# A two-layer hybrid trunk: the attention's queries and keys are projected with channels in the rows

## Chip, cores and metric

One of the eight cores of a Trainium2 chip runs the whole program. The metric is the device time of one execution in microseconds (us).

## What is computed

The input is 256 positions of 2048 channels. Each of two layers normalises it, projects it once to 7692 columns, and gives slices of the result to three mixers: a gated convolution module (31 taps, layer norm, a 512x512 projection), a gated DeltaNet with 6 heads, and an attention with 12 heads of 64 channels. The concatenated outputs go through one output projection and are added to the residual. The change concerns the attention's queries and keys:

```python
x1, x2, rest = x[..., :8], x[..., 8:16], x[..., 16:]          # per head, x is q or k
x = concatenate([x1 * c - x2 * s, x2 * c + x1 * s, rest])     # c, s: tables by position
s = einsum("qe,ke->qk", q, k) * 64 ** -0.5
```

Only 16 of a head's 64 channels are rotated, channel j with channel j+8.

## The kernel before

**Main chain.** All large projections are one sequence of jobs (`project`, line 466), run one after the other on TensorE. A job multiplies 16 blocks of 128 input channels; a block is a `unit` (line 439). Weights arrive as f32 (`raw`), ScalarE rounds them to a high part (`whi`, line 191), VectorE forms the low part (`wlo`, line 199), and each unit adds three products. There are two ways to place a unit. With `chan` false the activations (`HT`) are the stationary operand and the weight rows stream: 6 matmuls of 384 columns for a 384 wide block, the result has positions in the rows. With `chan` true the weights are stationary and the 256 positions stream: 9 matmuls of 256 columns, the result has channels in the rows. Three slots hold `whi` and three hold `wlo`, one for each chunk of two units.

**Order of jobs in a layer**: decay columns and DeltaNet keys, conv inputs, DeltaNet queries, values and gate, then for each half i of the heads attention queries, keys and values (AQ, AK, AV), then the conv gate (CG, 512 columns), the conv module's own projection (`wpw`, 4 units; its `then` is `conv_out`), the attention gates (AG), and the output projection.

**Everything else** is small tasks, interleaved with the chain. Small matmuls and transposes write to four PSUM tiles, `MIX` (named mix0 to mix3, also 123 to 126), which a task gets and puts back. `Plan` (line 70) is a list scheduler that runs when the program is built: with estimated costs it takes, of all tasks, the one that can start first, and on a tie the one with the lowest priority number. It fixes the order of every engine's instructions, and each engine then runs in that order. Attention pairs (`att_pair`) have priority 16, the conv module (`conv_a`) 20.

**The conv module** runs on VectorE for most of a layer (31 taps x 4 blocks). When the last tap is done, a chain follows: four transposes per half of the positions (`trs`, line 239), copies with sums and squares with sums on ScalarE, a power on GpSimd (`gpow`, line 248), scaling on VectorE, eight transposes back, scale, tanh and product, and the split into YT, which the `wpw` job reads.

**Queries and keys** (`heads_in`): the 384 columns come with positions in the rows and are scaled by `rstd` (or `half` for q) as they leave PSUM. VectorE rotates the 16 channels per head with four small operations per half of the positions, TensorE turns three blocks of 128 channels with two transposes each, and ScalarE copies the result.

Of the kernel before, what the change touches and what calls it, by code (L numbers as in the profile page):

```python
# [11 lines left out]
F32 = mybir.dt.float32  # L12
# [3 lines left out]
ALU = mybir.AluOpType  # L16
# [5 lines left out]
S = 256  # L22
DEPTH = 2
H = 6
AH = 12
HD = 64
CW = 31
KB = D // 128
NT = S // 128
# [4 lines left out]
AQ, AK, AV, AG = 4620, 5388, 6156, 6924  # L34
# [6 lines left out]
P_CW, P_DW, P_DB, P_LW, P_LB, P_GN, P_AL, P_DT, PCOLS = 16, 88, 212, 216, 220, 224, 225, 231, 237  # L41


PAD = (32, 16)


class Event:
# [128 lines left out]
def hybrid_trunk(ctx, tc, x, x_t, w_in, conf_pw_w, w_out, params, final_norm_w, rope, lnc, out):  # L176
    nc = tc.nc
    cp = ctx.enter_context(tc.tile_pool(name="consts", bufs=1))
# [5 lines left out]
    plan = Plan()  # L184


    def act(out_, in_, func=AF.Copy, scale=1.0, bias=0.0, accum=None):
        n_ap = sum(not isinstance(v, (int, float)) for v in (scale, bias)) + (accum is not None)
        kw = {} if accum is None else {"accum_out": accum}
        return ("act", 95 + _free(out_) / 1.2 + 93 * n_ap,  # L190
                lambda: nc.scalar.activation(out_, in_, func, bias=bias, scale=scale, **kw))  # L191
# [44 lines left out]
    def trs(*jobs):  # L236
        def emit():
            for o, a in jobs:
                nc.tensor.transpose(o, a, ident)  # L239
        return ("pe", 107.0 * len(jobs), emit)  # L240
# [14 lines left out]
        return Slots([(pool or sp).tile([128, cols], dt, name=f"{name}{i}", tag=f"{name}{i}") for i in range(n)])  # L255

    lncs = cp.tile([128, 384], F32, name="lncs")
    ropes = cp.tile([128, NT, 32], F32, name="ropes")
    cp.tile([128, PAD[0]], F32, name="pad0")
    HT = [cp.tile([128, KB, S], F32R, name=f"HT{i}") for i in range(2)]  # L260
    YT = [cp.tile([128, KB, S], F32R, name=f"YT{i}") for i in range(2)]
# [5 lines left out]
    S768 = many(14, 768, "b768_")  # L267
# [4 lines left out]
    S256 = many(4, 256, "b256_")  # L272
# [3 lines left out]
    MIX = many(4, 512, "mix", pool=pp)  # L276
# [29 lines left out]
    RSTD = [cp.tile([128, NT], F32, name=f"rstd{l}") for l in range(DEPTH + 1)]  # L306
    sums = cp.tile([128, NT], F32, name="sums")
    cp.tile([128, PAD[1]], F32, name="pad1")
    HALF = [cp.tile([128, NT], F32, name=f"half{l}") for l in range(DEPTH)]
    ROW = [cp.tile([128, S], F32, name=f"row{l}") for l in range(DEPTH)]  # L310
    misc_ready = [Event() for _ in range(DEPTH)]
    conv_ready = [Event() for _ in range(DEPTH)]
# [68 lines left out]
    def load_x(j):  # L381

        c0, n = X_PIECES[j]
        buf = yield ("get", S768)
        xs = buf[:, :NT * n].rearrange("p (t c) -> p t c", t=NT)
        yield ("dma", 128 * NT * n * 4 / 330.0, lambda: nc.sync.dma_start(
            xs, xf[:, c0:c0 + n].rearrange("(t p) c -> p t c", p=128)))
        plan.spawn(sums_x(j, xs, buf), 3)
        if j == len(X_PIECES) - 1:
            nc.sync.dma_start(lncs, lnc)  # L390
            nc.sync.dma_start(ropes, rope.rearrange("(t p) c -> p t c", p=128))

    def sums_x(j, xs, buf):
        yield from square_sums(0, j, [xs[:, t] for t in range(NT)], nsq0[j])
# [113 lines left out]
    rstd_ready = [Event() for _ in range(DEPTH)]  # L508
    final_ready = [Event() for _ in range(NT)]
    row_ready = [Event() for _ in range(DEPTH)]  # L510

    def square_sums(l, j, xs, ev):
        for t in range(NT):
# [35 lines left out]
    def finish_norm(l, evs, t0=0, t1=NT):  # L549
        for e in evs:  # L550
            yield ("wait", e)
        r = RSTD[l][:, t0:t1]
        if l == DEPTH:
            yield ts(r, SSQ[l][:, t0:t1, len(LAST_PIECES) - 1], 1.0 / D, sums[:, t0:t1], ALU.mult, ALU.add)
        else:
            yield ("dve", 90.0, lambda: nc.vector.tensor_reduce(r, SSQ[l][:, t0:t1], AX.X, ALU.add))
            yield ts(r, r, 1.0 / D, 1e-6, ALU.mult, ALU.add)
        yield gpow(r, r, pw_neg[:, :t1 - t0])
        if l == DEPTH:
            yield ("set", final_ready[t0])  # L560
            return
        yield ts(HALF[l], r, 0.125, None, ALU.mult)
        yield ("set", rstd_ready[l])
        ps = yield ("get", MIX)
        yield trs(*((ps[:, t * 128:(t + 1) * 128], r[:, t:t + 1].to_broadcast([128, 128])) for t in range(NT)))
        yield copy(ROW[l], ps[:, :S])
        yield ("put", MIX, [ps])
        yield ("set", row_ready[l])


    def layer(l):
        par = PAR[l]
        cw, dw = par[:, P_CW:P_CW + 72], par[:, P_DW:P_DW + 4 * CW]
        rstd, half = RSTD[l], HALF[l]
        y_ready = [Event() for _ in range(KB)]
        jobs = []

        def evac(acc, n, dsts, scale=None):
            yield ("wait", rstd_ready[l])
            for t in range(NT):  # L580
                yield act(dsts[t], acc[t][:, :n], scale=(rstd if scale is None else scale)[:, t:t + 1])


        conf = {k: Event() for k in ("pw", "b", "g")}
# [240 lines left out]
        def keys():  # L825
            for h in range(H):
                yield ("wait", gd["head"]["k", h])
            yield ("wait", gd["g"])
            yield ts(ssk, ssk, 4e-6, None, ALU.add)
            yield gpow(rk, ssk, pw_neg)  # L830
            yield tt(ivk, ssk, rk, ALU.mult)
            yield tt(fm, rk, rk, ALU.mult)
            yield tt(fm, fm, be.rearrange("p t h -> p (t h)"), ALU.mult)
            yield tt(ko, fm[:, :H], eg[:, 0], ALU.mult)
            yield ("set", gd["f"])
# [190 lines left out]

        at, at_have = {}, {(w, i): Event() for w in "qk" for i in range(2)}

        def heads_in(which, i):
            def then(acc):  # L1030
                raw = yield ("get", S768)
                tl = raw.rearrange("p (t c) -> p t c", t=NT)
                sc = rstd if which != "q" else half
                yield from evac(acc, 384, [tl[:, t] for t in range(NT)], sc)
                yield ("put", ACC, [acc])
                if which == "v":
                    at["v", i] = tl
                    for hp in range(3):
                        plan.spawn(att_pair(i, hp), 16 + 0.1 * hp)
                    return  # L1040
                ra, rb = yield ("get", S256, 2)
                ra_, rb_ = (r[:, :96].rearrange("p (h e) -> p h e", e=16) for r in (ra, rb))
                for t in range(NT):
                    v = tl[:, t].rearrange("p (h e) -> p h e", e=HD)
                    cc = ropes[:, t:t + 1, 0:16].to_broadcast([128, 6, 16])
                    ns = ropes[:, t:t + 1, 16:24].to_broadcast([128, 6, 8])
                    ss = ropes[:, t:t + 1, 24:32].to_broadcast([128, 6, 8])
                    yield tt(ra_, v[:, :, 0:16], cc, ALU.mult)
                    yield tt(rb_[:, :, 0:8], v[:, :, 8:16], ns, ALU.mult)
                    yield tt(rb_[:, :, 8:16], v[:, :, 0:8], ss, ALU.mult)  # L1050
                    yield tt(v[:, :, 0:16], ra_, rb_, ALU.add)
                yield ("put", S256, [ra, rb])
                buf = yield ("get", S768)
                dst = buf.rearrange("p (h s) -> p h s", s=S)
                for b in range(3):
                    ps = yield ("get", MIX)
                    yield trs(*((ps[:, t * 128:(t + 1) * 128], tl[:, t, b * 128:(b + 1) * 128])
                                for t in range(NT)))
                    yield act(dst[:, b, :], ps[:, :S])
                    yield ("put", MIX, [ps])  # L1060
                yield ("put", S768, [raw])
                at[which, i] = dst
                yield ("set", at_have[which, i])
            return then

        def att_pair(i, hp):
# [169 lines left out]
        def inp(c0, n, then, prio, chan=False):  # L1236
            order = full if l or jobs else halved
            jobs.append((HT, h_ready[l], win, c0, n, order, then, prio, None, chan))
# [7 lines left out]
                inp(c0 + 384 * i, 384, gdn_block(w, i), 6, True)  # L1246
        inp(GZ, 384, z_block, 6)
        for i in range(2):
            for w, c0 in (("q", AQ), ("k", AK), ("v", AV)):
                inp(c0 + 384 * i, 384, heads_in(w, i), 7)  # L1250
        inp(CG, 512, conv_gate, 6, True)
        cs_ready = [conf["pw"]] * KB
        jobs.append((YT, cs_ready, wpw, 0, 512, full[:2], conv_out, 6, None, True))
# [2 lines left out]
        for j, (c0, n) in enumerate(pieces):  # L1256
            mode = "last" if last and j == len(pieces) - 1 else False
            jobs.append((YT, y_ready, wout, c0, n, [(4 * i, 4) for i in range(4)] if mode else full, (last_residual if last else residual)(j),
                         4, load_residual(j), mode))
        bg = [(keys(), 11), (gdn_out(), 13)] + [(scores(b), 14) for b in range(4)] + [(state(i), 12) for i in range(2)]  # L1260
        return jobs, bg

    setup_consts()
# [38 lines left out]
def _rope_table():  # L1302

    half = 8
    inv = np.float32(500000.0) ** (-np.arange(half, dtype=np.float32) / np.float32(half))
    ang = np.arange(S, dtype=np.float32)[:, None] * inv.astype(np.float32)[None, :]
    c, s = np.cos(ang), np.sin(ang)
    return np.concatenate([c, c, -s, s], axis=1).astype(np.float32)


def _pattern_logs():
# [26 lines left out]
```

## Time and profile before

| what | value |
|---|---|
| median of 3 runs | 972.93 us (972.45 to 974.32) |
| the profiled execution | 972.88 us, its span 971.2 us |
| TensorE matmul busy | 958.6 us, 99% of the span |
| VectorE busy | 748.1 us, 77% |
| ScalarE busy | 550.8 us, 57% |
| GpSimd busy | 48.6 us, 5% |
| granted TensorE clock | 0.997 of full |

Matmul spans overlap their neighbours, so the busy share alone does not say how fast the columns flow. The chain of waits gives a number of matmuls and the time from the first to the last of a stretch, and that quotient is the cost of one.

### The profile page before, as it was taken

The numbers are of one execution on the slowest core, as the hardware profiler recorded it, in microseconds if no ns is written. First come the engines' busy times: TensorE is split into PE (matmuls) and PEld (weight loads), VectorE is DVE, ScalarE is ACT, GpSimd is POOL, SyncE is SP. The second block draws the span as 40 slices with busy tenths as digits, with TensorE's granted clock in tenths as the row PEclk, the third lists the DMA queues.
The fourth block names the chain that finished last, engine by engine and source line by source line (L and its number), as shares of the span: only waits on it lengthen the run. The fifth ranks groups of instructions, "written<-read, shape, count | busy, mean of one in ns | idle before, by whom it ended". The sixth has DMA issues, their size and how long they took to land.

```text
span 971.2 us, 19060 instructions
## 1 busy us (share of the span) xinstructions
PE 958.6 (99%) x7259; PEld 937.3 (97%) x7259; DVE 748.1 (77%) x1519; ACT 550.8 (57%) x1079; POOL 48.6 (5%) x70
## 2 busy tenths in 40 slices
PE   8999999999999999999999999999999999999996
PEld 8999999999999999999899999999899999999996
DVE  7697799999999666655558768999999976666672
ACT  7774355446685764554456634564466767544551
POOL 1002100200010000000000020002000100000000
PEclk9999999999999999999999999999999999999998
DMA  9865565644445535776666555556344556467772
GB/s 325 261 201 170 175 192 183 187 148 146 148 138 173 183 114 185 222 244 219 215 194 196 196 168 172 188 181 196 123 149 142 151 186 203 125 194 218 221 252 88
DMA packets 67037, 179.01 MB, mean 184 GB/s; under 512 B 8000, under 2 KB 12224, under 8 KB 66944
## 3 DMA queue, kind: packets, MB, share of 16 engines
q1 hardware_dynamic: 64880, 173.85, 55.6%
q0 software_dynamic: 1632, 3.02, 1.2%
q8 instruction: 57, 0.93, 0.4%
q10 hardware_dynamic: 432, 0.91, 0.3%
q14 instruction: 36, 0.29, 0.1%
HBM read 172.77 MB, written 4.98 MB: 183 GB/s over the span
## 4 chain that ended last, share of the span: by engine, by line
PE 97%; DVE 1%; DMA 1%; issue 1%; SPq 0%; ACT 0%; POOLq 0%; POOL 0%; DVEq 0%; ACTq 0%
PE acc L455 87%; PE mix L232 6%; PE mix L239 3%; DMA b<-in_x_t 1%; PE acc L464 1%; PE mix L754 0%; DVE wlo L199 0%; DVE b L196 0%; SPq L411 0%; SPq L369 0%; DVE inv L212 0%; ACT whi L191 0%; POOLq L1334 0%; POOL rstd L248 0%; DVE PTs L206 0%
## 5 line engine op out<-in xcount | busy, mean ns | idle before, releaser
L191 ACT ACTIVATE whi<-raw 128x768 fp32r<-128x768 f32 (+4 forms) x389 | 339.9, 874 | 352.5 <-PE acc L455 313.0
L199 DVE TENSOR_TENSOR wlo<-raw,whi 128x768 fp32r<-128x768 f32 (+4 forms) x389 | 385.2, 990 | 178.9 <-ACT whi L191 174.8
L455 PE MATMUL acc<-HT,whi 128*128 128x256 f32 x2304 | 404.7, 280 | 0.0
L455 PEld LDWEIGHTS acc<-HT,whi 128*128 128x128 f32 x2304 | 350.4, 189 | 1.5 <-issue 1.5
L455 PE MATMUL acc<-HT,wlo 128*128 128x256 f32 x1152 | 320.5, 278 | 0.0
L455 PE MATMUL acc<-whi,HT 128*128 128x384 f32 (+1 forms) x1024 | 270.8, 346 | 1.1 <-ACT whi L191 1.1
L455 PEld LDWEIGHTS acc<-HT,wlo 128*128 128x128 f32 x1152 | 216.3, 188 | 0.0
L455 PEld LDWEIGHTS acc<-whi,HT 128*128 128x128 f32 x1024 | 180.2, 189 | 3.4 <-ACT whi L191 1.5
L455 PE MATMUL acc<-wlo,HT 128*128 128x384 f32 (+1 forms) x512 | 173.1, 338 | 0.6 <-DVE wlo L199 0.6
L455 PE MATMUL acc<-whi,YT 128*128 128x384 f32 (+2 forms) x640 | 161.8, 336 | 0.0
L196 DVE SCALAR_TENSOR_TENSOR b<-b,par,b 128x255 f32<-128x255 f32 (+20 forms) x348 | 153.6, 465 | 0.3
L455 PEld LDWEIGHTS acc<-whi,YT 128*128 128x128 f32 x640 | 113.9, 188 | 2.4
L455 PE MATMUL acc<-wlo,YT 128*128 128x384 f32 (+2 forms) x320 | 107.5, 336 | 0.0
L455 PEld LDWEIGHTS acc<-wlo,HT 128*128 128x128 f32 x512 | 96.3, 188 | 1.6 <-DVE wlo L199 1.6
L455 PEld LDWEIGHTS acc<-wlo,YT 128*128 128x128 f32 x320 | 60.1, 188 | 1.4
L191 ACT ACTIVATE b<-mix 128x384 f32<-128x384 f32 (+3 forms) x96 | 39.6, 425 | 19.2 <-PE mix L232 12.3
L232 PE MATMUL mix<-b,b 128*128 128x128 f32 (+5 forms) x456 | 45.9, 285 | 0.0
L239 PE MATMUL mix<-ident,b 128*128 128x128 f32 x280 | 45.8, 274 | 0.0
L232 PEld LDWEIGHTS mix<-b,b 128*128 128x128 f32 (+3 forms) x456 | 36.2, 161 | 6.6 <-issue 2.2
L239 PEld LDWEIGHTS mix<-ident,b 128*128 128x128 f32 x280 | 34.1, 141 | 3.8 <-issue 1.3
L196 DVE SCALAR_TENSOR_TENSOR b<-b,b 128x256 f32<-128x256 f32 (+3 forms) x62 | 31.5, 510 | 2.5 <-ACT b L191 2.3
L191 ACT ACTIVATE b<-b,stat 128x128 f32<-128x128 f32 (+1 forms) x68 | 29.1, 442 | 6.0 <-DVE stat L206 5.9
(146 smaller groups left out, 612.9 us busy)
## 6 DMA issues: line engine op xcount, KB each, us to landing
raw<-in_w_in SPq DMA_DIRECT2D x240, 384.0 KB, 3.0
raw<-in_w_in SPq DMA_DIRECT2D x48, 512.0 KB, 3.9
raw<-in_w_out SPq DMA_DIRECT2D x64, 384.0 KB, 3.5
raw<-in_w_out SPq DMA_DIRECT2D x12, 512.0 KB, 4.1
raw<-in_w_in SPq DMA_DIRECT2D x15, 396.0 KB, 3.7
b<-in_x SPq DMA_DIRECT2D x10, 256.0 KB, 5.4
raw<-in_conf_pw_w SPq DMA_DIRECT2D x4, 512.0 KB, 3.2
raw<-in_w_out SPq DMA_DIRECT2D x8, 256.0 KB, 3.6
```

The costliest lines, as they stand in the source:

```text
L191: lambda: nc.scalar.activation(out_, in_, func, bias=bias, scale=scale, **kw))
L196: lambda: nc.vector.scalar_tensor_tensor(out_, a, s, b, op0=op0, op1=op1))
L199: return ("dve", 70 + _free(out_) / 0.96, lambda: nc.vector.tensor_tensor(out_, a, b, op=op))
L232: nc.tensor.matmul(o, a, b, start=f[0], stop=f[1])
L239: nc.tensor.transpose(o, a, ident)
L455: nc.tensor.matmul(o, w, m, start=first and i == 0 and not (chan and t % 2), stop=last and i == 2, skip_group_check=chan)
L464: nc.tensor.matmul(acc[t][:, :n], YT[w][:, k, s], HT[m][:, k, :n], start=k == 0 and i == 0, stop=k == KB - 1 and i == 2)
```

## The change

Queries and keys become `chan` jobs: 9 matmuls of 256 columns per unit in place of 6 of 384, and the result already has channels in the rows, so that their six transposes per job and the three copies behind them go. The scale by `rstd` moves into the rotation tables: `rope_rows` multiplies tables of [128, 2, 256] (cosine and signed sine by channel, one and zero for channels that are not rotated) by the row of `rstd`; in the second layer the tables are first loaded again, on GpSimd's queue. The partner channel is fetched by four DMAs of eight partitions each, issued from ScalarE, into a second buffer that GpSimd has cleared. VectorE then does three operations of 768 elements per job. Paddings change so that later buffers keep their places. The new table is built on the host.

```diff
@@ constants and buffers
-PAD = (32, 16)
+PAD = (96, 28)
-    ropes = cp.tile([128, NT, 32], F32, name="ropes")
+    ropes = cp.tile([128, 2, S], F32, name="ropes")
-    HALF = [cp.tile([128, NT], F32, name=f"half{l}") for l in range(DEPTH)]
-            nc.sync.dma_start(ropes, rope.rearrange("(t p) c -> p t c", p=128))
+            nc.sync.dma_start(ropes, rope)
+    rope_free = [Event() for _ in range(DEPTH)]
@@ finish_norm
-        yield ts(HALF[l], r, 0.125, None, ALU.mult)
@@ layer
-        def heads_in(which, i):
+        def rope_rows():
+
+            yield ("wait", row_ready[l])
+            if l:
+                yield ("wait", rope_free[l - 1])
+                yield ("pool", 3500.0, lambda: nc.gpsimd.dma_start(ropes, rope))
+            yield tt(ropes, ropes, row[:, None, :].to_broadcast([128, 2, S]), ALU.mult)
+            yield ("set", rope_ready)
+
+        rope_ready = Event()
+
+        def heads_in(i):
             def then(acc):
                 raw = yield ("get", S768)
                 tl = raw.rearrange("p (t c) -> p t c", t=NT)
...
-                ra, rb = yield ("get", S256, 2)
-                ra_, rb_ = (r[:, :96].rearrange("p (h e) -> p h e", e=16) for r in (ra, rb))
-                for t in range(NT):
-                    v = tl[:, t].rearrange("p (h e) -> p h e", e=HD)
-                    cc = ropes[:, t:t + 1, 0:16].to_broadcast([128, 6, 16])
-                    ns = ropes[:, t:t + 1, 16:24].to_broadcast([128, 6, 8])
-                    ss = ropes[:, t:t + 1, 24:32].to_broadcast([128, 6, 8])
-                    yield tt(ra_, v[:, :, 0:16], cc, ALU.mult)
-                    yield tt(rb_[:, :, 0:8], v[:, :, 8:16], ns, ALU.mult)
-                    yield tt(rb_[:, :, 8:16], v[:, :, 0:8], ss, ALU.mult)
-                    yield tt(v[:, :, 0:16], ra_, rb_, ALU.add)
-                yield ("put", S256, [ra, rb])
-                buf = yield ("get", S768)
-                dst = buf.rearrange("p (h s) -> p h s", s=S)
-                for b in range(3):
-                    ps = yield ("get", MIX)
-                    yield trs(*((ps[:, t * 128:(t + 1) * 128], tl[:, t, b * 128:(b + 1) * 128])
-                                for t in range(NT)))
-                    yield act(dst[:, b, :], ps[:, :S])
-                    yield ("put", MIX, [ps])
...
+        def rotated(which, i):
+
+
+            def then(acc):
+                buf, sh = yield ("get", S768, 2)
+                sc = 0.125 if which == "q" else 1.0
+                yield act(buf[:, :512], acc[0], scale=sc)
+                yield act(buf[:, 512:], acc[1][:, :S], scale=sc)
+                yield ("put", ACC, [acc])
+                yield ("pool", 800.0, lambda: nc.gpsimd.memset(sh, 0.0))
+
+                def emit():
+                    for p in (0, 64):
+                        nc.scalar.dma_start(sh[p:p + 8], buf[p + 8:p + 16])
+                        nc.scalar.dma_start(sh[p + 8:p + 16], buf[p:p + 8])
+                yield ("dma", 300.0, emit)
+                yield ("wait", rope_ready)
+                b3, s3 = (b.rearrange("p (h s) -> p h s", s=S) for b in (buf, sh))
+                for v, part in ((b3, 0), (s3, 1)):
+                    yield tt(v, v, ropes[:, part:part + 1, :].to_broadcast([128, 3, S]), ALU.mult)
+                yield tt(buf, buf, sh, ALU.add)
+                yield ("put", S768, [sh])
...
-            for w, c0 in (("q", AQ), ("k", AK), ("v", AV)):
-                inp(c0 + 384 * i, 384, heads_in(w, i), 7)
+            for w, c0 in (("q", AQ), ("k", AK)):
+                inp(c0 + 384 * i, 384, rotated(w, i), 7, True)
+            inp(AV + 384 * i, 384, heads_in(i), 7)
...
-        bg = [(keys(), 11), (gdn_out(), 13)] + [(scores(b), 14) for b in range(4)] + [(state(i), 12) for i in range(2)]
+        bg = [(rope_rows(), 13), (keys(), 11), (gdn_out(), 13)] + [(scores(b), 14) for b in range(4)] + [(state(i), 12) for i in range(2)]
```

The scheduler gives another order after the change. On TensorE in the first layer, before (`b_0_104` is the conv module's result, `b_0_107` and `b_1_108` its normalised halves, `b_3_93` an attention query; the last row is the first matmul of the `wpw` job):

```order
L239 MATMUL mix_123<-ident,b_0_104 128x128 x4
L239 MATMUL mix_124<-ident,b_12_102 128x128 x2
...
L239 MATMUL mix_125<-ident,b_0_104 128x128 x4
...
L232 MATMUL mix_126<-b_3_93,b_6_96 128x128
...
L239 MATMUL mix_124<-ident,b_0_107 128x128
...
L239 MATMUL mix_125<-ident,b_0_107 128x128
...
L455 MATMUL acc_129<-YT_76,whi_85 128x256
```

The conv module's result is turned ahead of the score matmuls of the second half of the heads, and 228 projection matmuls (6 units of AV and all 16 of CG) stand between its second group and `wpw`.

The same place on TensorE after the change:

```order
L239 MATMUL mix_125<-ident,b_0_109 128x128 x3
L239 MATMUL mix_126<-ident,b_1_110 128x128 x3
...
L232 MATMUL mix_126<-b_12_102,b_5_95 128x128
...
L239 MATMUL mix_124<-ident,b_0_104 128x128 x4
...
L239 MATMUL mix_125<-ident,b_0_104 128x128 x4
...
L239 MATMUL mix_126<-ident,b_2_111 128x128 x3
...
L239 MATMUL mix_124<-ident,b_0_107 128x128
...
L239 MATMUL mix_125<-ident,b_0_107 128x128
...
L454 MATMUL acc_129<-YT_76,whi_85 128x256
```

The conv module's result is now turned behind two attention pairs, 36 projection matmuls (3 units of CG) ahead of `wpw`, and the transposes back stand directly ahead of `wpw`'s first matmul. The second layer has the same order there.

On VectorE in the first layer, the last taps of the conv module before (`b_12_102` with `ropes` is the rotation of a key; `wlo` splits belong to AV and, from `wlo_88<-raw_78`, to its last chunk):

```order
L199 TENSOR_TENSOR b_2_117<-b_12_102,ropes 128x6x8
L196 SCALAR_TENSOR_TENSOR b_0_104<-b_1_105,par_149,b_0_104 128x226
L199 TENSOR_TENSOR wlo_86<-raw_80,whi_83 128x768
L199 TENSOR_TENSOR b_2_117<-b_12_102,ropes 128x6x8
...
L199 TENSOR_TENSOR b_12_102<-b_3_118,b_2_117 128x6x16
L199 TENSOR_TENSOR wlo_87<-raw_81,whi_84 128x768
L199 TENSOR_TENSOR wlo_88<-raw_78,whi_85 128x768
L206 TENSOR_SCALAR lnst_3555<-lnst_3555 128x2
```

And after (L244 is an attention pair's maximum, `wlo` of 1024 elements belongs to CG):

```order
L199 TENSOR_TENSOR b_12_102<-b_12_102,b_3_93 128x768
...
L199 TENSOR_TENSOR wlo_88<-raw_78,whi_85 128x768
L196 SCALAR_TENSOR_TENSOR b_0_104<-b_1_105,par_149,b_0_104 128x229 x3
L199 TENSOR_TENSOR wlo_86<-raw_79,whi_83 128x1024
...
L244 ISA b_1_110,stat_137<-mix_126,lncs 128x256
...
L196 SCALAR_TENSOR_TENSOR b_0_104<-b_1_105,par_149,b_0_104 128x226 x3
L199 TENSOR_TENSOR wlo_88<-raw_80,whi_85 128x1024
```

Sixteen of the 124 tap operations have moved behind the last weight split of AV, the last six of them behind the maxima of two attention pairs.

## Rows read from the trace of the kernel before

**Rows 1.** The page: span, and TensorE's busy time, share and instructions.
```profile
span 971.2 us, 19060 instructions
PE 958.6 (99%) x7259; PEld 937.3 (97%) x7259; DVE 748.1 (77%) x1519; ACT 550.8 (57%) x1079; POOL 48.6 (5%) x70
```
**Rows 2.** The chain that ended last: shares of the span by engine.
```profile
PE 97%; DVE 1%; DMA 1%; issue 1%; SPq 0%; ACT 0%; POOLq 0%; POOL 0%; DVEq 0%; ACTq 0%
```
**Rows 3.** Waits: engine and line, waited for; us, times, longest.
```profile
ACT whi L191 <- PE acc L455: 313.0, 277, 3.4
```
**Rows 4.** The chain in order of time: start us, us, what.
```profile
305.05 0.22 PE mix L239 x2
338.98 2.74 PE acc L455 x24
...
93.72 41.50 PE acc L455 x366
...
412.84 16.64 PE acc L455 x96
...
569.62 44.52 PE acc L455 x378
```
**Rows 5.** Groups by shape on VectorE and ScalarE: count, busy us, mean ns, idle before.
```profile
L199 DVE TENSOR_TENSOR wlo<-raw,whi 128x768 fp32r<-128x768 f32 x304 | 290.5, 955 | 114.0 <-ACT whi L191 110.4
...
L199 DVE TENSOR_TENSOR wlo<-raw,whi 128x1024 fp32r<-128x1024 f32 x60 | 73.4, 1224 | 50.6 <-ACT whi L191 50.3
L191 ACT ACTIVATE whi<-raw 128x1024 fp32r<-128x1024 f32 x60 | 63.7, 1061 | 57.4 <-PE acc L455 56.7
...
L199 DVE TENSOR_TENSOR b<-b,ropes 128x48 f32<-128x48 f32 x32 | 6.3, 200 | 0.0
...
L199 DVE TENSOR_TENSOR b<-b,ropes 128x96 f32<-128x96 f32 x16 | 4.0, 250 | 0.0
```
**Rows 6.** Windows: length, busy of PE, PEld, DVE, ACT, POOL; clock, DMA.
```profile
218.20:240.80 22.60, 22.60 (x153) 22.50 (x151) 21.11 (x51) 13.99 (x34) 0.00 (x0) 1.00 0.45 144
```
**Rows 7.** Timelines of PE, ACT, DVE, POOL at the conv chain, first layer.
```profile
316.17 0.82 PE L239 MATMUL mix<-ident,b 128*128 128x128 f32 x6
...
317.78 0.20 ACT L191 ACTIVATION_READ_ACCUMULATOR b<-mix 128x1 f32 x1
...
320.22 0.71 ACT L191 ACTIVATE JUNK<-b,lnst 128x512 bf16<-128x512 f32 x1
...
321.50 0.16 DVE L208 TENSOR_SCALAR lnst<-lnst 128x2 f32<-128x2 f32 x1
...
321.74 0.70 POOL L248 TENSOR_TENSOR lnst<-lnst,pw_neg 128x2 f32<-128x2 f32 x1 [48.25 <-DVE lnst L208]
...
323.47 0.99 DVE L208 TENSOR_SCALAR b<-b,lnst 128x512 f32<-128x512 f32 x2
...
343.80 1.02 ACT L191 ACTIVATE b<-mix,par 128x256 f32<-128x256 f32 x2 [0.27 <-PE mix L239]
344.86 0.63 ACT L191 ACTIVATE b<-b 128x512 f32<-128x512 f32 x1
...
348.16 0.69 DVE L199 TENSOR_TENSOR YT<-b,YT 128x512 fp32r<-128x512 f32 x1
...
352.30 0.39 PE L455 MATMUL acc<-YT,whi 128*128 128x256 f32 x2
```
**Rows 8.** Windows at the end of the span, columns as in rows 6.
```profile
962.00:963.00 1.00, 0.88 (x8) 0.67 (x6) 0.09 (x1) 0.00 (x0) 0.00 (x0) 1.00 0.69 276
...
965.00:966.00 1.00, 0.00 (x0) 0.00 (x0) 0.93 (x2) 0.85 (x1) 0.00 (x0) 0.66 0.00 0
```
**Rows 9.** Single lines (duration ns min/median/max, starts) and TensorE's first row (start, us).
```profile
L1228 ACTq DMA_DIRECT2D out<-b x2: 366/372/379, 960.2 to 965.9; - x2
...
1.58 3.46 PE L318 MATMUL mix<-ident,ones 128*128 128x128 f32 x15 [1.58 <-POOL pw_neg L323]
...
L881 POOL MEMSET inv<- x2: 975/976/977, 102.4 to 576.3; 48x1024 f32 x2
```

More of the change, by code (lines that the diff above doesn't have):

```diff
@@ L573, in layer, with evac @@
         cw, dw = par[:, P_CW:P_CW + 72], par[:, P_DW:P_DW + 4 * CW]
-        rstd, half = RSTD[l], HALF[l]
+        rstd = RSTD[l]
         y_ready = [Event() for _ in range(KB)]
         jobs = []
-        def evac(acc, n, dsts, scale=None):
+        def evac(acc, n, dsts):
             yield ("wait", rstd_ready[l])
             for t in range(NT):
-                yield act(dsts[t], acc[t][:, :n], scale=(rstd if scale is None else scale)[:, t:t + 1])
+                yield act(dsts[t], acc[t][:, :n], scale=rstd[:, t:t + 1])
         conf = {k: Event() for k in ("pw", "b", "g")}
@@ L1032, in then @@
                 tl = raw.rearrange("p (t c) -> p t c", t=NT)
-                sc = rstd if which != "q" else half
-                yield from evac(acc, 384, [tl[:, t] for t in range(NT)], sc)
+                yield from evac(acc, 384, [tl[:, t] for t in range(NT)])
                 yield ("put", ACC, [acc])
[L1036 to L1040, printed above, removed]
@@ L1052, in then @@
-                yield ("put", S256, [ra, rb])
-                buf = yield ("get", S768)
-                dst = buf.rearrange("p (h s) -> p h s", s=S)
-                for b in range(3):
-                    ps = yield ("get", MIX)
-                    yield trs(*((ps[:, t * 128:(t + 1) * 128], tl[:, t, b * 128:(b + 1) * 128])
-                                for t in range(NT)))
-                    yield act(dst[:, b, :], ps[:, :S])
-                    yield ("put", MIX, [ps])
-                yield ("put", S768, [raw])
@@ L1062, in then @@
-                at[which, i] = dst
+                at["v", i] = tl
+                for hp in range(3):
+                    plan.spawn(att_pair(i, hp), 16 + 0.1 * hp)
+            return then
+        def rotated(which, i):
[17 more added lines that the diff above has]
+                yield ("put", S768, [sh])
+                at[which, i] = b3
@@ L1063, in then @@
                 yield ("set", at_have[which, i])
+                at["rot"] = at.get("rot", 0) + 1
+                if at["rot"] == 4:
+                    yield ("set", rope_free[l])
             return then
@@ L1306, in _rope_table @@
     ang = np.arange(S, dtype=np.float32)[:, None] * inv.astype(np.float32)[None, :]
-    c, s = np.cos(ang), np.sin(ang)
-    return np.concatenate([c, c, -s, s], axis=1).astype(np.float32)
+    c, s = np.cos(ang).T, np.sin(ang).T
+    t = np.zeros((128, 2, S), np.float32)
+    t[:, 0] = 1.0
+    for p in (0, 64):
+        t[p:p + 16, 0] = np.concatenate([c, c])
+        t[p:p + 16, 1] = np.concatenate([-s, s])
+    return t
 def _pattern_logs():
```

## The prediction

> **What bounds the kernel now.** I read the page first: TensorE is busy for 958.6 of 971.2 us, 99% [rows 1]. Since busy matmul spans overlap, I then took the chain of waits: 97% of it is TensorE, and no other engine has more than 1% [rows 2]. The list of waits says the same from the other side: ScalarE waits 313.0 us for TensorE to free a weight slot [rows 3], so the weight splits run ahead. A change therefore moves the time only by what TensorE executes, or by a place where TensorE has to wait and did not before. VectorE deserves a look all the same: in the attention projections it is busy for 21.11 of 22.60 us [rows 6], so there its queue is full and whatever has the lowest priority, the conv module, comes last.
>
> **The change part by part.** All sums are made against the profiled execution, 972.88 us with a span of 971.2, which agrees with the median of 972.93.
>
> *Transposes removed.* Six per job, four jobs a layer, two layers: 48. A pair takes 0.22 us of the chain [rows 4], so one costs 0.11 and all cost 48 x 0.11 = 5.3 us. They stand on TensorE, which never waits there, so they come off the path: **-5.3**.
>
> *Projections in the other form.* A unit with positions in the rows is 6 matmuls at 16.64/96 = 173.3 ns, 1040 ns [rows 4]. With channels in the rows it is 9 matmuls, for which the chain shows 41.50/366 = 113.4 ns in one stretch, 44.52/378 = 117.8 in another, and 2.74/24 = 114.2 in CG, between small matmuls [rows 4]. So 9 of them take 1021, 1060 or 1028 ns. There are 16 x 8 = 128 units, so the difference is -2.5, +2.6 or -1.6 us. The attention jobs are as full of small matmuls as CG, so I take CG's rate: **-1.6**, with -2.5 and +2.6 as bounds. A rule speaks against this part: the Trainium skill (TensorE: Matmul & The Clock Gate, the section on 56 ns in place of 53.3) gives each warm matmul a fixed cost of about 2.5 ns beside its columns. By that alone three more matmuls a unit would cost 128 x 3 x 2.5 ns, an estimate of about 1 us, and the whole sum would come out 2.6 us later. The rows above disagree: per column 256 wide matmuls are here no dearer than 384 wide ones.
>
> *VectorE.* Rotation was eight small operations per job, four of 48 elements at 200 ns and four of 96 at 250 [rows 5], 1.8 us. Now it is three operations of 768 elements; the nearest row of that size is a weight split of 955 ns [rows 5], so 2.9 us. Each job adds 1.1 us, and the table product about 0.7 a layer (the 512 element subtraction takes 0.69 [rows 7]). That is 5 us a layer, not on the path by itself, but in the stretch in which VectorE is full, and it is the conv module that yields. Own price 0; its consequence is the wait below.
>
> *ScalarE, GpSimd, DMA.* Per job three copies and two scalings go and two copies come; four DMA issues come, each holding ScalarE's queue for 372 ns by the nearest row [rows 9], together 1.5 us. Behind them stand weight splits, which are covered as long as the delay is shorter than ScalarE's idle time before them, up to 3.4 us [rows 3]. GpSimd clears a buffer in about 1 us (1024 elements: 976 ns [rows 9]); the DMA issues wait for that, but the clearing starts when its buffer is free, ahead of the job's end. A job of 16.6 us follows before the rotated tensor is wanted. Price 0; if the cover failed at each job, 1.5 us x 8 = 12.
>
> *The wait that the new order adds.* This is the largest term. In the order after the change, two attention pairs take all four MIX tiles when CG begins, and the last taps of the conv module stand behind their maxima on VectorE. So its transposes come only when the pairs put the tiles back, 36 projection matmuls ahead of `wpw`, where before there were 228. `wpw` reads the conv module's result, TensorE goes in order, and no projection may pass. What is the chain from the second group of transposes to the first matmul of `wpw`, and what covers it?
>
> The chain before, in the first layer: from the start of that group at 316.17 to the end of the two scalings on VectorE at 323.47 + 0.99 = 324.46 it took 8.3 us [rows 7], with the sums, the squares, GpSimd's power of 0.70 and the scalings in between. The group held two foreign transposes, less 0.2. Four transposes back and the hand-over: 0.44 + 0.27 [rows 7] = 0.7. From the two scalings on ScalarE at 343.80 to the end of the split at 348.16 + 0.69 = 348.85: 5.05 us [rows 7]. Together 13.8 us. Before, this ended 3.4 us ahead of `wpw` at 352.30 [rows 7], though it began 36 us ahead.
>
> The cover after: 36 matmuls x 114.2 ns = 4.1 us, and 22 small matmuls (the group itself, one attention pair's, eight transposes back) x 0.11 = 2.4. So TensorE waits 13.8 - 6.5 = 7.3 us. The second layer has the same order: **+14.6**. Bounds: between those steps of before stood weight splits, two on each engine by 1.06 and 1.22 us [rows 5], 4.6 in all. Were none in the way, the chain would be 9.2 and the wait 2.7 a layer, 5.4 in all. Upwards, the order after puts three operations of the conv gate (two of 512 and one of 1024 elements, 0.69 x 2 + 1.22 = 2.6) ahead of the last steps on VectorE: 9.9 a layer, 19.8 in all. I stay with the chain as it was measured, because the new order has weight splits between the same steps again.
>
> *The clock.* After the last matmul, which ends within 962 to 963, the granted clock is at full for about a third of 965 to 966 and then at half (0.66 in that row [rows 8]): it fell from 2.4 to 1.2 GHz some 2.4 us after work ended. The new wait is of that size or longer, broken up by small matmuls. Each fall would make the following matmuls take twice their time: at the start of the span, 15 transposes took 3.46 us [rows 9], 0.23 each against 0.11 later, so such a stretch loses about 1.7. Nothing to four such falls, 0 to 6.8; I take **+1.0**, since the gaps are broken.
>
> **Sum:** 972.88 - 5.3 - 1.6 + 14.6 + 1.0 = 981.6 us, slower by 0.9%.
>
> **Rivals.**
> (a) *The wait is short, and the result is no change or a gain.* If the engines take the chain at its own durations, 2.7 us a layer, it is 972.88 - 6.9 + 5.4 = 971.4; with no wait at all, 966.0. For it: VectorE and ScalarE have little else to do while TensorE stands. Against it: in the order the weight splits and the conv gate's operations stand ahead of the chain's steps. It decides at 3.45 us a layer, that is a chain of about 10 us.
> (b) *The clock falls at each wait.* Two broken waits a layer, 6.8 us in place of 1.0: 987.4. For it: the fall at the end of the span after 2.4 us. Against it: small matmuls inside the wait.
> (c) *ScalarE stalls at the DMA issues.* The partner copy waits for GpSimd, whose queue holds the DeltaNet's powers; weight splits behind it come late. At 1.5 us each, 8 times: 981.6 + 12 = 993.6. Against it: in the order the clearings stand ahead of or just behind the powers, a job's length early.
> (d) *Projections at the slow rate*, 117.8: +4.2, so 985.8.
>
> **How the numbers follow.** A measurement of this kernel can tell about 0.2%, 2 us, from no change. The forecast (976 to 986) has 0.62, (a) 0.19, of which 0.08 is a gain of over 2 us and 0.11 no change, (b) 0.10, (c) 0.03, (d) 0.06 beyond what the forecast covers. The range goes from 971.5, where (a)'s gains begin, to 988, above (b). Faster 0.08, same 0.11, slower 0.81.
>
> **What would show it.** In the changed kernel: 48 fewer transposes at line 238 (their line moves up by one); chain stretches of 256 columns at 113 to 118 ns in the AQ and AK jobs; in the chain of waits TensorE's share below 97% and, twice, around the first matmul of `wpw`, ScalarE, VectorE and GpSimd pieces of 7 us together; idle time of TensorE ended by VectorE or ScalarE there and nowhere else. Wrong would be: no gap ahead of `wpw` (then the time is near 966), gaps in the AQ to AV jobs (then the partner copy or VectorE is late), or a granted clock below 1.00 in more than those stretches.

## The result: the changed kernel is 1.1% slower

| | before | after |
|---|---|---|
| median of 4 runs each | 972.99 us (972.45 to 974.32) | 983.36 us (981.83 to 985.56) |
| ratio after to before | | 1.0107 (95%: 1.0088 to 1.0125) |
| profiled execution, its span | 972.88, 971.2 us | 983.13, 981.4 us |
| granted TensorE clock | 0.997 | 0.991 |

The forecast was 981.6 us, its range 971.5 to 988.0. The page after, to be read against [rows 1] and [rows 2]; `PEclk` is the granted clock in 40 slices of the span, in tenths:

```profile
span 981.4 us, 19748 instructions
PE 959.3 (98%) x7595; PEld 937.9 (96%) x7595; DVE 758.6 (77%) x1473; ACT 544.7 (56%) x1061; POOL 57.4 (6%) x79
...
PEclk9999999999999979999999999999999999999998
...
PE 60%; DVE 1%; ACT 1%; issue 1%; ACTq 0%; POOLq 0%; POOL 0%; DVEq 0%
```

Two things are new. One slice, near 343 to 368 us, has a lowered clock. And the chain of waits, which was TensorE for 97%, can be followed back from the end only to 353 us, the place that the forecast named; TensorE's share of the span in it is 60%, because the first 353 us are missing from it: of the 628 us that it covers, TensorE has 94%. Its two longest pieces (start us, us, what):

```profile
359.13 59.74 PE acc L454 x443
...
848.22 113.39 PE acc L454 x791
```

Both begin inside a `wpw` job. What stands there, first layer, TensorE's timeline (start us, us, engine, line, operation, count, idle before and its releaser):

```profile
344.59 0.60 PE L239 MATMUL mix<-ident,b 128*128 128x128 f32 x4
...
349.01 0.28 PE L454 MATMUL acc<-HT,wlo 128*128 128x256 f32 x1
352.25 0.48 PE L239 MATMUL mix<-ident,b 128*128 128x128 f32 x1 [2.97 <-DVE b L206]
353.01 2.24 PE L239 MATMUL mix<-ident,b 128*128 128x128 f32 x9 [0.28 <-ACT b L191]
355.18 1.54 PE L232 MATMUL mix<-b,b 128*64 128x256 f32 x8
356.66 1.11 PE L239 MATMUL mix<-ident,b 128*128 128x128 f32 x4
358.41 1.31 PE L454 MATMUL acc<-YT,whi 128*128 128x256 f32 x2 [0.64 <-ACT YT L191]
```

The first row is the second group of the conv module's transposes, the last the first matmul of `wpw`. The last projection matmul of CG starts at 349.01, and at 113 ns each the next could start at 349.12. The next, `wpw`'s first, starts at 358.41, 9.3 us later, with 22 small matmuls in between. At 0.11 us these would take 2.4 us, so 6.9 us are lost. The second layer has the same picture:

```profile
835.42 0.28 PE L454 MATMUL acc<-HT,wlo 128*128 128x256 f32 x1
837.87 0.33 PE L239 MATMUL mix<-ident,b 128*128 128x128 f32 x1 [2.17 <-DVE b L208]
839.64 1.99 PE L239 MATMUL mix<-ident,b 128*128 128x128 f32 x9 [1.44 <-DVE b L208]
841.71 2.03 PE L232 MATMUL mix<-b,b 128*64 128x256 f32 x8
843.67 0.66 PE L239 MATMUL mix<-ident,b 128*128 128x128 f32 x4
844.09 0.54 PE L454 MATMUL acc<-YT,whi 128*128 128x256 f32 x2
```

844.09 less 835.53 is 8.6, less 2.4 is 6.1 us. Some 40% of the time lost is not idle time (3.9 and 3.6 us are, by the gaps above) but mostly small matmuls at the slow clock, as windows of the first layer show (columns as in [rows 6]; the clock is the third number from the end):

```profile
350.00:352.00 2.00, 0.00 (x0) 0.00 (x0) 2.00 (x5) 0.86 (x3) 1.35 (x1) 0.94 0.61 206
352.00:354.00 2.00, 1.46 (x6) 0.98 (x7) 1.82 (x4) 1.86 (x5) 0.00 (x0) 0.50 0.55 187
...
360.00:362.00 2.00, 2.00 (x11) 2.00 (x11) 1.30 (x2) 0.63 (x1) 0.00 (x0) 0.50 0.00 0
362.00:364.00 2.00, 2.00 (x19) 2.00 (x18) 0.54 (x2) 0.85 (x1) 0.00 (x0) 1.00 0.00 0
```

TensorE fell from 2.4 to 1.2 GHz as the wait went on, and stayed there through the small matmuls and the first 14 of `wpw`'s 48: 11 matmuls in 2 us, then 19. In the kernel before, the clock was full there.

### The profile page after: what moved, and what is told of

It is laid out like the page before. It is cut to its first block, busy times and chain, and to the rows that moved or that the text cites. A ratio compares the mean times of both kernels' runs of the same rounds, so it can differ in the third digit from the quotient of the medians.

```text
span 981.4 us, 19748 instructions
## 1 busy us (share of the span) xinstructions
PE 959.3 (98%) x7595; PEld 937.9 (96%) x7595; DVE 758.6 (77%) x1473; ACT 544.7 (56%) x1061; POOL 57.4 (6%) x79
## 4 chain that ended last, share of the span: by engine, by line
PE 60%; DVE 1%; ACT 1%; issue 1%; ACTq 0%; POOLq 0%; POOL 0%; DVEq 0%
PE acc L454 54%; PE mix L232 3%; PE mix L239 2%; PE acc L463 1%; ACT b L191 0%; DVE b L196 0%; DVE wlo L199 0%; ACT JUNK L191 0%; ACT whi L191 0%; ACT YT L191 0%; DVE YT L199 0%; PE mix L753 0%; DVE inv L212 0%; DVE b L199 0%; ACTq L1064 0%
## 5 line engine op out<-in xcount | busy, mean ns | idle before, releaser
L454 PE MATMUL acc<-HT,whi 128*128 128x256 f32 x3072 | 541.7, 280 | 0.0
L454 PEld LDWEIGHTS acc<-HT,whi 128*128 128x128 f32 x3072 | 466.4, 188 | 2.3 <-issue 1.8
L454 PE MATMUL acc<-HT,wlo 128*128 128x256 f32 x1536 | 426.7, 278 | 0.0
L454 PEld LDWEIGHTS acc<-HT,wlo 128*128 128x128 f32 x1536 | 288.6, 188 | 0.0
L454 PE MATMUL acc<-whi,HT 128*128 128x384 f32 (+1 forms) x512 | 134.6, 344 | 0.6 <-ACT whi L191 0.6
L454 PEld LDWEIGHTS acc<-whi,HT 128*128 128x128 f32 x512 | 91.8, 190 | 1.3 <-ACT whi L191 1.2
L454 PE MATMUL acc<-wlo,HT 128*128 128x384 f32 (+1 forms) x256 | 87.2, 341 | 0.4 <-DVE wlo L199 0.4
L454 PEld LDWEIGHTS acc<-wlo,HT 128*128 128x128 f32 x256 | 48.3, 189 | 1.1 <-DVE wlo L199 0.9
L191 ACT ACTIVATE b<-mix 128x384 f32<-128x384 f32 (+3 forms) x70 | 29.4, 436 | 16.9 <-PE mix L232 9.0
L191 ACT ACTIVATE JUNK<-b 128x128 bf16<-128x128 f32 (+3 forms) x62 | 25.0, 403 | 16.2 <-DVE b L199 11.0
```

Of the source, the lines that this page charges most:

```text
L454: nc.tensor.matmul(o, w, m, start=first and i == 0 and not (chan and t % 2), stop=last and i == 2, skip_group_check=chan)
```

## The experiments

The theory: the change takes some 6 us off TensorE's path and adds a wait ahead of `wpw`, because the conv module's last steps start too late to be covered. Rivals: the projections in the other form, the rotation's work or the DMA issues cost the time; or the slow clock does.

**wpw moved behind both attention gates** in the changed kernel (and conv rows read last by the first output piece, so that its result is not wanted at once):

```
-        jobs.append((YT, cs_ready, wpw, 0, 512, full[:2], conv_out, 6, None, True))
         for i in range(2):
             inp(AG + 384 * i, 384, att_gate(i), 6, True)
+        jobs.append((YT, cs_ready, wpw, 0, 512, full[:2], conv_out, 6, None, True))
...
-   ... if mode else full, (last_residual
+   ... if mode else full if j else full[2:] + full[:2], (last_residual
```

> The changed kernel with the wpw job moved behind both attention gates, and the first output piece reading the conv rows of YT last; nothing is left out, the same work is done. In its order the second group of the conv module's transposes still stands where it stood (36 projection matmuls ahead of the end of CG), but 324 projection matmuls lie between it and the first matmul of wpw, in place of 36. Theory (the loss is the wait ahead of wpw, with the slow clock behind it): the wait is covered, and what is left is 972.9 - 5.3 - 1.6 = 966.0; up to 968 if the stretch of the attention projections gives less than the sum says, as its job times suggest. Rival (the projections in the other form, the rotation on VectorE or the DMA issues on ScalarE cost TensorE the time, wherever wpw stands): 981 to 983, as the changed kernel. No idle time of TensorE over 0.5 us between 330 and 400 us by the theory, and a granted clock of 1.00 there.

Measured: 967.36 us (966.06 to 968.40), ratio to before 0.9940 (0.9926 to 0.9953). The same work, 16.0 us less than the changed kernel, and faster than before. Its windows at the place:

```profile
336.00:346.00 10.00, 10.00 (x93) 9.08 (x93) 5.76 (x15) 5.48 (x13) 0.00 (x0) 1.00 0.46 147
346.00:356.00 10.00, 10.00 (x90) 10.00 (x90) 7.08 (x13) 8.84 (x21) 0.69 (x1) 1.00 0.30 83
356.00:366.00 10.00, 10.00 (x90) 9.56 (x89) 5.26 (x8) 6.34 (x11) 0.00 (x0) 1.00 0.61 173
```

TensorE is busy throughout and at full clock. So the place of one job decides whether the change is a loss or a gain, and the projections, the rotation and the copies, which are all still there, are not the cause.

**The same move in the kernel before**, as a control.

> The kernel before with the wpw job moved behind both attention gates, in the same way as in the changed kernel with that move. Theory: before, nothing waited ahead of wpw, so the move is worth nothing by itself: 972.9 (971.5 to 974). Rival (the move is a gain of its own, by other weight order or rates): 967 to 969, and then the moved changed kernel says nothing about the change.

Measured: 972.65 us (972.24 to 974.03), ratio 0.9998 (0.9989 to 1.0006). The move is worth nothing where nothing waits.

**The kernel with wpw moved, conv module at another priority** (16.15 in place of 20).

> The changed kernel with wpw moved behind both attention gates and, besides, the conv module's job given a priority between the second and the third attention pair (16.15 in place of 20). The order puts both of its first groups of transposes together, 12 matmuls earlier. Theory: nothing waits there any more, so it is the same as with the move alone, 967.4 (966 to 968.4). Rival (VectorE's order there still costs): 965 or less.

Measured: 967.86 us (966.57 to 968.37): no difference. Once the wait is covered, a place 12 matmuls earlier for the conv module is worth nothing; other places were not tried.

**wpw moved behind the first attention gate only.**

> The changed kernel with the wpw job moved behind the first attention gate only. In its order 180 projection matmuls lie between the second group of conv transposes and wpw in both layers (20.5 us against a chain of 13.8), but the last group of transposes back stands only 27 and 36 ahead in the two layers (3.1 and 4.1 us). Theory: no wait for the chain as a whole; the steps behind the last transposes (5.8 us of the chain) are covered by 3.1 and 4.1 us and by half of wpw, which reads the first half of YT first (2.7 us): 967.4 as with the move behind both gates, up to 969.5. Rival (the wait is set by the planner's place of the back transposes, not by the start of the chain): 971 to 973.

Measured: 969.35 us (967.99 to 970.50), 2.0 us above the move behind both, within the theory's range. The part that is left is in the first layer, inside `wpw`, where the second half of YT is late:

```profile
372.06 0.38 PE L454 MATMUL acc<-YT,whi 128*128 128x256 f32 x1 [0.83 <-ACT YT L191]
373.06 0.38 PE L454 MATMUL acc<-YT,whi 128*128 128x256 f32 x1 [0.62 <-DVE YT L199]
```

So a cover of 180 matmuls ahead of the chain suffices for its first part, but the 27 behind the last transposes do not quite cover the last steps. Each step of such a chain needs its own cover.

**Only one attention pair at a time may hold MIX tiles** until the conv module's first transposes are done (`conf["tr"]` is set there), in the changed kernel with wpw where it was:

```
+            if i == 1 and hp >= 1:
+                yield ("wait", conf["tr"])
             qT, kT, v = at["q", i], at["k", i], at["v", i]
```

> The changed kernel in which the second and third attention pair of the second head group wait, in the planner, until the conv module's first transposes are done; nothing is left out. Only one pair can then hold MIX tiles (two of four) when CG begins. In its order the second group of conv transposes stands 72 projection matmuls ahead of wpw in the first layer and 156 in the second, in place of 36 and 36. Theory (the pairs' hold on the four MIX tiles is what keeps the conv module back, and the wait is its chain of 13.8 us less the matmuls ahead): the cover grows by 4.1 us in the first layer and by more than the wait in the second, but the attention pairs that now come last wait in their turn, 1 to 2 us in each layer: 983.4 - 4 - 6 + 3 = 976.4 (973 to 979). Rival (the tiles don't matter, only VectorE's late taps do): 982 to 985.

Measured: 976.59 us (974.78 to 977.64), ratio 1.0031 (1.0020 to 1.0042): 6.8 us less than the changed kernel, as the theory had it. The attention pairs ahead of the conv module are thus a part of why it came late. Whether they hold it up by the four MIX tiles or by their maxima ahead of the last taps on VectorE is not shown: the edit holds back a pair as a whole, its maxima with it. The granted clock was 1.00 in both places, and what is left is the cover that is still too short, in the second layer a transpose's wait of

```profile
835.26 1.17 PE L239 MATMUL mix<-ident,b 128*128 128x128 f32 x6 [2.39 <-ACT b L191]
```

and in the first layer five waits of 0.2 to 0.4 us between 350 and 360 us, for VectorE and ScalarE.

**No partner copies** in the changed kernel (the loop with the four `nc.scalar.dma_start` left out).

> The changed kernel without the four copies of eight partitions (the clearing and the three VectorE operations stay), so the partner rows stay zero and the output differs. In its order the first layer is as in the changed kernel (second group of the conv transposes 36 projection matmuls ahead of wpw), but in the second layer that group stands 156 ahead, the transposes back 60 and 12. Theory (the wait ahead of wpw is the loss, and goes where the order covers it; the copies have no price): the first layer keeps its wait, the second loses most of it. The changed kernel loses 16.0 us to both layers against the kernel with wpw moved behind the gates, that is about 8 us a layer, so 983.4 - 7 = 976.4 (974.5 to 977.5, as 12 matmuls don't cover the last steps in the second layer). Rival (the DMA issues on ScalarE's queue hold up weight splits or the attention everywhere): both layers gain alike, and TensorE's gaps go from AQ to AV; by 1.5 us a job it would be 971.4.

Measured: 977.64 us (975.59 to 979.19). The median is just above the theory's 974.5 to 977.5, a narrow miss, and far from the rival's 971.4. The layer whose order has not changed keeps its wait, and the other has a shorter one, but still one:

```profile
351.34 0.37 PE L239 MATMUL mix<-ident,b 128*128 128x128 f32 x1 [2.98 <-DVE b L206]
...
836.48 1.73 PE L239 MATMUL mix<-ident,b 128*128 128x128 f32 x6 [2.39 <-ACT b L191]
```

I had counted too little for the second: the wait was followed by a slow clock there as well (from 838.44 us on the first matmuls of `wpw` are 0.21 us apart). This run also takes 1.7 us of waits out of the attention jobs (below), so the two effects are mixed in it.

**No rotation** in the changed kernel: no table, clearing, copies or VectorE operations for queries and keys.

> The changed kernel without the rotation: the table, its product, the clearing, the four copies of eight partitions and the three VectorE operations of each job are left out, so that queries and keys are not rotated and the output differs; the projections keep the new form. In its order the conv module's second group of transposes stands 240 and 276 projection matmuls ahead of wpw, in place of 36 and 36. Theory (rotation has no price of its own, only that VectorE's load pushes the conv module behind the pairs): 966.0, the same as the kernel with wpw moved. Rival one (the rotation's work costs TensorE time of its own): clearly below the kernel with wpw moved, by 1.1 us a job or more, that is by 9 us or more. Rival two (the other form of the projections is what costs): no better than 981.

Measured: 966.68 us (966.35 to 967.42). Without that load on VectorE the planner puts the conv module early again, and the wait is gone: behind the start of the span TensorE's longest wait in its trace is 0.55 us. Against the kernel with wpw moved, which does rotate, it is 0.7 us less, with overlapping ranges: the rotation has next to no price of its own.

**Old form of the projections, nothing behind them**: the kernel before with wpw moved, without rotation, transposes and copies.

> The kernel before with wpw moved behind both attention gates, and without the rotation, the transposes of queries and keys and their copies (left out, the output differs): the projections with positions in the rows and no work behind them. To be set against the changed kernel without the rotation (966.7), which has the projections with channels in the rows and no work behind them. Theory: 972.9 less the transposes, 4.9 by the doubled ones, is 968.1, so that the other form is worth -1.4, where the sum had -1.6 (bounds -2.5 and +2.6). Rival (the other form costs, by a fixed cost for each matmul): 964 to 966.

Measured: 967.14 us (966.91 to 967.25). The other form is 0.5 us less (966.68); the ranges overlap, so that its sign is not settled, but 1 us more is outside of them. The theory's 968.1 was 1.0 too high: against the kernel before with only the move (972.65), leaving out rotation, transposes and copies gives 5.5 us, 0.6 more than the transposes' 4.9, and where that 0.6 comes from stays open. The chain of the kernel without rotation shows both rates of 256 columns in the AQ and AK jobs:

```profile
197.78 3.08 PE acc L454 x27
...
220.54 3.18 PE acc L454 x27
```

114.1 and 117.8 ns.

**Transposes of queries and keys twice** in the kernel before, in the same order.

> The kernel before with every transpose of queries and keys executed twice, 48 more in all, in the same order of everything else. Theory (they stand on TensorE's path, 0.11 us each): 972.9 + 5.3 = 978.2. Rival (they lie beside waits or are hidden by the matmuls around them): 972.9 to 974.

Measured: 977.99 us (977.53 to 978.08), ratio 1.0049 (1.0037 to 1.0062): 4.9 us for 48 transposes, 0.10 each of the 0.11 expected. Nearly all of their time is on the path.

**A gap filled with matmuls** in the changed kernel, for the clock. Nobody reads them; they stand ahead of all that waits:

```
             acc = yield ("get", ACC)
+            if w[0] is conf_pw_w:
+                n_fill = 26 if c0_fill.pop() else 19
+                yield ("pe", 1.0, lambda: [nc.tensor.matmul(acc[0][:, :S], HT[0][:, 0, 0:128], HT[0][:, 0, :], start=True, stop=True,
+                                                            skip_group_check=True) for _ in range(n_fill)])
```

> The changed kernel with matmuls that nobody reads put into TensorE's queue right behind the last projection of CG: 26 in the first layer and 19 in the second, of 256 columns, 113 ns each, that is 2.9 and 2.2 us, the length of the first gap there; everything else stands in the same order. Theory (part of the loss is the clock that falls after the gap): the granted clock stays at 1.00 in the first layer's stretch, the small matmuls and those of wpw run at full rate, and the chain behind them comes earlier: about 2.6 us less in the first layer (wpw ends 1.3 us earlier for the small matmuls and as much again for its own), 0.5 in the second, where a second gap of 1.4 us stays: 980.3. Rival (the clock costs nothing, since TensorE waits for the chain anyway): 983.4, and more if the added matmuls are late themselves.

Measured: 982.79 us (981.60 to 984.41), ratio to before 1.0101 (1.0087 to 1.0114). That is 0.6 us less than the changed kernel, within the intervals: my theory of 980.3 fell, and the rival is close. The clock did stay up, until a later wait:

```profile
352.00:354.00 2.00, 1.50 (x11) 0.96 (x10) 2.00 (x4) 2.00 (x5) 0.00 (x0) 1.00 0.68 195
354.00:356.00 2.00, 2.00 (x15) 1.42 (x16) 0.60 (x2) 1.37 (x4) 0.00 (x0) 1.00 0.00 2
...
360.00:362.00 2.00, 2.00 (x12) 2.00 (x11) 0.90 (x2) 0.64 (x2) 0.00 (x0) 0.50 0.00 0
```

and the small matmuls ran fast, but then `wpw` waited for the chain:

```profile
353.23 1.57 PE L239 MATMUL mix<-ident,b 128*128 128x128 f32 x9 [0.43 <-ACT b L191]
...
357.96 0.38 PE L454 MATMUL acc<-YT,whi 128*128 128x256 f32 x1 [1.43 <-ACT YT L191]
```

From the nine transposes to `wpw` it is 4.73 us here and 5.40 in the changed kernel (353.01 to 358.41), 0.7 less; in the second layer 3.9 (838.07 to 841.97) and 4.45, 0.55 less. Inside a wait a slow clock mostly fills time that would be idle. What it costs in `wpw` itself the run does not test in the first layer, since the clock fell there in both kernels.

## Why the prediction was right, step by step

**The wait: the right mechanism and place, and nearly the right size.** It was +14.6. By the rows it is 6.9 + 6.1 = 13.0 us ahead of `wpw`, where it had 7.3 twice. The chain from the second group of transposes to the first matmul of `wpw`, forecast at 13.8 from [rows 7], took 13.8 in the first layer (344.59 to 358.41). The cover was counted a little short: the 22 small matmuls in it were to include the second group itself, but 22 stand behind CG and the group's four come on top. With 26 the same sum gives 13.8 - 4.1 - 2.9 = 6.8 us a layer, nearer to the 6.9 and 6.1 measured.

The chain's parts did not come out: errors of both signs cancelled. To the end of the two scalings on VectorE,

```profile
352.11 0.54 DVE L208 TENSOR_SCALAR b<-b,lnst 128x512 f32<-128x512 f32 x1
...
355.29 1.02 ACT L191 ACTIVATE b<-mix,par 128x256 f32<-128x256 f32 x2 [1.01 <-PE mix L239]
...
357.72 0.63 ACT L191 ACTIVATE YT<-b 128x512 fp32r<-128x512 f32 x1 [0.49 <-DVE b L196]
358.38 0.69 DVE L199 TENSOR_TENSOR YT<-b,YT 128x512 fp32r<-128x512 f32 x1 [0.69 <-ACT YT L191]
```

it took 8.06 (forecast 8.1). The transposes back and their hand-over took 2.64 to 355.29, in place of 0.7: six transposes of an attention pair stood ahead of them in TensorE's queue, waiting in their turn for VectorE and ScalarE, and ran at the slow clock. From there to `wpw` it took 3.1 in place of 5.05. Of that difference 0.7 is a step that the forecast put ahead of `wpw`'s first matmul and that only the second one waits for, the low part of YT on VectorE (last line above, done at 359.07). The other 1.3: the weight splits that I had kept between the steps were not there; ScalarE's next one, at 362.61, waits for TensorE to free a slot. Rival (a) was right about that part.

The second layer does not have quite the same order. There the first four transposes back stand ahead of the pair's six, and the first half of YT is rounded by 843.46, before TensorE comes to `wpw` at 844.09: what it was still at are the pair's own matmuls (841.71 in the rows above, 2.03 us for eight).

**The clock: too small.** The term was +1.0, a guess between 0 and 6.8. Windows at half clock cover some 10 us of the first layer and 3 of the second, far more than the broken gaps seemed to allow. `wpw` takes 7.65 us in the first layer (358.41 to 366.06), where 48 matmuls of 113.4 ns are 5.4. Of the 2.2 us more, some 0.8 is the second matmul's wait for the low part of YT, and some 1.3 is the slow clock: from the second matmul to the fifteenth, at 362.06, the matmuls stand 0.21 us apart. In the second layer `wpw` takes 1.4 us more, at full clock, with waits of 0.7 for the second half of YT inside.

Filling the gap gave 0.6 us, but in the first layer the clock fell all the same, inside `wpw`. The kernel without partner copies says more. Of its six runs two had a mean clock of 0.997 and took 975.59 and 975.65 us; the other four had 0.991 to 0.993 and took 977.42 to 979.19. Its trace is of one of the four (978.74 us), and its half clock covers the same 10 and 3 us as in the changed kernel. So in one and the same order the runs in which the clock fell are 1.8 to 3.6 us longer. No edit tested that the fall is the cause, but the estimate of +1.0 lies below. The slow small matmuls are counted in the 13.0 us of the wait, so that only the sum of the two terms can be compared: by rows wait and `wpw` make 13.0 + 3.6 = 16.6, the medians of the changed kernel and of the one with wpw moved differ by 16.0, and the forecast was 14.6 + 1.0 = 15.6. A wait taken too long and a clock taken too cheap thus made up for each other.

**Transposes: right.** 48 fewer:

```profile
L239 PE MATMUL mix<-ident,b 128*128 128x128 f32 x232 | 39.4, 290 | 7.2 <-DVE b L208 3.6 <-DVE b L206 3.0 <-DVE YT L196 0.3
```

against 280 before (they stay at line 239; the forecast said 238). Worth 4.9 by the doubled ones, at most 5.5 by leaving them out with all that stands behind them; forecast 5.3.

**Projections: a little too good.** Forecast -1.6, measured -0.5, within the bounds of -2.5 and +2.6. The step that failed was to take one rate of CG for all of them, when stretches of both rates alternate. The remark that 256 wide matmuls are no dearer per column than 384 wide ones holds at 113.4 ns (0.443 ns a column against 0.451) and not at 117.8 (0.460). A rule of the Trainium skill (TensorE: Matmul & The Clock Gate, the section on 56 ns in place of 53.3) would have given an estimate of +1.0; that is 967.14 + 1.0 = 968.1 for the kernel without rotation, outside of its 966.35 to 967.42.

**VectorE, ScalarE, GpSimd: price nearly 0, as forecast**, but not "idle there and nowhere else". The three operations are 950 ns each as estimated, the clearing 740 instead of 976. The copies hold ScalarE's queue for 632 ns each, and not 372 [rows 9]:

```profile
L199 DVE TENSOR_TENSOR b<-b,ropes 128x768 f32<-128x768 f32 x16 | 15.2, 951 | 1.9 <-DMA b<-b 1.4 <-issue 0.4
...
L1063 ACTq DMA_DIRECT2D b<-b x16: 631/632/1230, 239.8 to 793.0; - x16
...
244.00 0.94 PE L232 MATMUL mix<-b,b 128*128 128x128 f32 x6 [0.97 <-ACT b L191]
```

The last row is the place where it shows: an AV job waits 0.97 us for a copy on ScalarE that stood behind four issues. With 0.31 and 0.40 elsewhere that makes 1.7 us of rival (c)'s 12. The kernel with wpw moved has these waits too, and one more: a partner copy issued at 784.28 lands 5.5 us later, VectorE stands for it, and TensorE waits for the weight split behind.

```profile
789.94 0.96 DVE L199 TENSOR_TENSOR b<-b,ropes 128x768 f32<-128x768 f32 x1 [2.70 <-DMA b<-b]
...
792.19 0.45 PE L454 MATMUL acc<-wlo,HT 128*128 128x384 f32 x1 [0.94 <-DVE wlo L199]
```

So rival (c) is real in kind, by VectorE as well as by ScalarE, but small: the kernel without rotation has none of these waits and is 0.7 us faster.

**Together.** With its own wait covered the change is worth 973.12 - 967.36 = 5.8 us, where the sum had 6.9 and a price of nothing for the rest. Of the signs named, GpSimd's pieces are missing from the chain of waits; ScalarE's and VectorE's are there, 3.3 us behind 353 us in the first layer and 7.4 ahead of 839.6 in the second. The total came out 1.8 us from the forecast, and part of that closeness is luck, the cancelling above.

## What to carry to other kernels

In a statically ordered kernel, a change that takes a little off one engine and puts a little on another can move a long chain of short steps on the others to a place where nothing covers it. Before such a change is judged, count for each step of the chain, the last ones too, how many instructions of the bound engine stand between it and its reader in the new order, and compare their time with the chain's. If the cover is short, move the reader: here that turned a loss of 1.1% into a gain of 0.6%, with all of the change kept.

## What the runs showed of the hardware

- Four copies of 8 partitions x 768 elements each held ScalarE's queue for 632 ns at the issue, against 372 for the output's DMAs.
- The clock fell in a stretch with one gap of 2.97 us followed by small matmuls, and in the first layer of the kernel with filled gaps also after shorter ones, the longest of 1.43 us, with small matmuls between them. In its second layer it stayed at 1.00 with gaps of up to 1.45 us. After one gap of 2.39 us in the second layer it fell in the kernel without partner copies (836.48) and stayed at 1.00 in the one with the pairs held back (835.26), so here the length of a gap alone does not decide.
- Matmuls of 256 columns run at 113.4 or at 117.8 ns for whole stretches, changing over at small matmuls and once, in the kernel with filled gaps, at a wait inside `wpw`. For the 288 matmuls of two AG jobs the two rates differ by 1.3 us, as much as the smaller terms of the sum.
